# Splitting the second FFN product's left operands in place, inside the last pair of the first product, with the stores between them on ScalarE's queue

## The chip, the cores and the metric

The kernel runs on one core of a Trainium2 chip. The metric is the time of one execution in device microseconds (us); each number below is a median of single executions or comes from the profile of one of them. The engines are named as the profile names them: PE is TensorE (matmuls), PEld its weight loads, DVE is VectorE, ACT is ScalarE, POOL is GpSimd and SP is SyncE, which only issues DMA transfers. "SPq" and "ACTq" are DMA issues of SP and ACT.

## The reference

One layer of an encoder over 1024 tokens of width 1024, all in float32:

```
xn = rmsnorm(h); proj = xn @ w_in
h  = h + concat(windowed attention(proj), gated DeltaNet(proj)) @ w_out
hn = rmsnorm(h)
h  = h + square(relu(hn @ w_ffn_in)) @ w_ffn_out      # 1024 -> 4096 -> 1024
out = rmsnorm(h)
```

Only the FFN line, the second from last, is touched by the change: the first product `hn @ w_ffn_in`, its activation, and the second product with `w_ffn_out`.

## The kernel before

*Arithmetic.* TensorE multiplies float32 through operands that are split in two: a high part, which ACT makes by a cast (L119), and a low part, raw minus high, which POOL or DVE makes by a subtraction (L120). One product is then three matmuls (`mm3`, L124 to L126): high by high, high by low, low by high. A matmul here is a 128 by 128 weight against 512 columns.

*Seven products instead of eight.* Both FFN products are cut in 2 by 2 blocks and done by a Strassen-Winograd scheme: seven block products P1 to P7 of sums and differences of the blocks, whose results are added up afterwards. `SECOND` gives the order in which the second product does them: P1, P2, P6, P5, P7, P3, P4.

*First product.* It runs over 16 pairs g (a pair is 256 of the 4096 hidden features). `columns` loads a pair's weights, forms their combinations on DVE (L1020 to L1028) and splits them. `pair_products` does the seven products, 12 matmuls each, so 84 a pair, against the normed tokens X, whose 28 split tiles (`B11`, `B21` and so on, four each) hold all 28 buffers of the pool `pg` until the last pair has used them. Results go from PSUM through ACT (copy, L1049) and DVE (additions, L1044) to the activation: relu and square on ACT (L1054, L1055). DVE then forms the left operands that the second product will want (L1098 to L1106), and `keep` (L1060) stores the seven of a pair to a tensor `sd` in device memory: 112 stores of 256 KB, issued by SP.

*Second product.* It runs over 4 chunks n (a chunk is four pairs k) times 7 products: 28 steps of 48 matmuls. `second_operands` prepares a step. For each k it loads the left operand from `sd` into a `pt` buffer (L1132), has ACT cast it and DVE subtract it into a `pg` tile, and forms and splits the right operand from `w_ffn_out`: the combinations T1 (L1137), T2 (L1139), T3 (L1142) and N4 (L1143) on DVE, the cast on ACT, the low part on POOL. `second_products` does the matmuls, in groups of 12 for each of four PSUM banks, and adds each bank to a tile of h (L1170). The tag `psA` has four banks, which P1 and P6 use, then P7 and P4, then the next chunk's P1; `psB` has the other four, for P2, P5 and P3.

*Buffers.* `pg` 28, `pt` 12, `wr` 4, `wh` 3, `wl` 3, `sc` 4 per partition, and a new tile waits until the one that had the buffer before was last used.

*The order of the work.* The code is written in program order, product by product; a scheduler then reorders the instructions of each engine by a simulated time line, and each engine works through its own list in order. So the emission order in Python is an input of the order on the chip, not the order itself. In the code before, the last pair (g = 15) is written whole, then `prepare(0)` (the operands of step 0), then eight loads of h, 512 KB each (L1308). From there each step is written behind the preparation of the next.

Of the kernel before, what the change touches and what calls it, by code (L numbers as in the profile page):

```python
# [9 lines left out]
F32 = mybir.dt.float32  # L10
F32R = mybir.dt.float32r
# [66 lines left out]
class Block:  # L78
# [979 lines left out]
    def keep(self, g, p, t):  # L1058

        self.nc.sync.dma_start(out=self.sd[g, SECOND.index(p)], in_=t)  # L1060
# [11 lines left out]
    def pair_products(self, g, ops):  # L1072
# [7 lines left out]
        self.keep(g, "P1", a11)  # L1080
        self.product(a, ops, "P6", False)
        u2 = self.copied(a)
        c = self.ps(tag)
# [12 lines left out]
        self.keep(g, "P4", a22)  # L1096
        s1, s2, s4 = self.pt(), self.pt(), self.pt()
# [13 lines left out]
    def load_second(self, n):  # L1111

        out = []
        for k in range(4):
            g = 4 * n + k
            r = []
            for i in range(2):
                t = (self.wr, self.wh, self.wl, self.sc)[(2 * k + i) % 4]((P, 2, HALF), F32)
                f = (2 * g + i) * P
                self.nc.sync.dma_start(out=t, in_=self.io["w_ffn_out"][0, f:f + P, :].rearrange("p (h c) -> p h c", h=2))  # L1120
                r.append(t)
            out.append({"B11": r[0][:, 0], "B12": r[0][:, 1], "B21": r[1][:, 0], "B22": r[1][:, 1]})
        return out

    def second_operands(self, n, w2, p):

        nc, v = self.nc, self.nc.vector
        left, right = [], []
        for k in range(4):
            b = w2[k]  # L1130
            raw = self.pt()
            nc.sync.dma_start(out=raw, in_=self.sd[4 * n + k, SECOND.index(p)])  # L1132
            s, t = self.pg((P, 2, HALF), F32R), self.pg((P, 2, HALF), F32R)
            self.split(raw, s[:, 0], s[:, 1], v)
            if p == "P6":
                b["T1"] = b["B11"]
                v.tensor_tensor(out=b["T1"], in0=b["B12"], in1=b["B11"], op=ALU.subtract)  # L1137
                b["T2"] = self.pt()
                v.tensor_tensor(out=b["T2"], in0=b["B22"], in1=b["T1"], op=ALU.subtract)  # L1139
            if p == "P5":  # L1140
                b["T3"], b["N4"] = b["B12"], b["B21"]
                v.tensor_tensor(out=b["T3"], in0=b["B22"], in1=b["B12"], op=ALU.subtract)  # L1142
                v.tensor_tensor(out=b["N4"], in0=b["B21"], in1=b["T2"], op=ALU.subtract)  # L1143
            self.split(b[SECOND_RIGHT[p]], t[:, 0], t[:, 1])
            left.append(s)
            right.append(t)
        return left, right

# [76 lines left out]
    def phases(self):  # L1225
# [60 lines left out]
        rest[0]("P6", "P5", "P4")  # L1286
        for g in range(ng):
            if g == 0:
# [3 lines left out]
            else:  # L1292
                w2 = self.load_second(0)
            self.pair_products(g, cols.pop(g))
        steps = [(n, p) for n in range(ng // 4) for p in SECOND]
        ops, banks = {}, {}

        def prepare(i):
            nonlocal w2
            n, p = steps[i]  # L1300
            if p == "P1" and n:
                w2 = self.load_second(n)
            ops[i] = self.second_operands(n, w2, p)

        prepare(0)
        for t in range(NT):
            self.h[t] = self.pg((P, D))
            nc.sync.dma_start(out=self.h[t], in_=self.hd[t])  # L1308
        self.u2 = [self.pg((P, 2, HALF)) for _ in range(2)]
        for i, (n, p) in enumerate(steps):  # L1310
            if i + 1 < len(steps):
                prepare(i + 1)
            last = n == ng // 4 - 1
# [24 lines left out]
```

## Time and profile before

| | |
|---|---|
| median of 3 runs | 1277.7 us (1276.8 to 1280.23) |
| profiled execution | 1276.97 us, span 1275.3 us, mean granted clock of TensorE 0.981 |
| busy, share of the span | PE 1207.9 us (95%), DVE 860.6 (67%), ACT 613.6 (48%), POOL 580.9 (46%) |
| last matmul of the first product starts / second product starts | 940.07 / 949.83 us |
| last matmul starts | 1266.57 us |

How to read it: the span runs from the first to the last instruction of the profiled execution, and all times are counted from its start. An engine with a share of 95% can bound the kernel only as long as it is busy; so the stretches in which it is not are what a change can win, or lose. "PEclk" is the clock that was granted to TensorE, as a part of full speed (1.00 is 2.4 GHz, 0.5 would be 1.2 GHz). A wait is written as who waited, in which line, for whom.

### The profile page before, as it was taken

Reading aid. Unit: us, or ns where it says so; the run is one execution under the profiler, and the core shown is the slowest. Engines: PE = TensorE matmul, PEld = TensorE weight load, DVE = VectorE, ACT = ScalarE, POOL = GpSimd, SP = SyncE. Lnnn points to the kernel's source line nnn. Section 1 sums busy time; section 2 is a strip of 40 time slices with the busy share of each in tenths; the row PEclk is TensorE's granted clock in tenths of the full one; section 3 lists DMA queues with packets and bytes.
Section 4 is the critical chain, followed back from the end, with each engine's and each line's share of the span. In section 5 each row is a group of like instructions: output and inputs, shape, how many; then the busy total and the mean of one; then the engine's idle time right before and its main releaser. Section 6 shows DMA issues by size and latency. Waiting matters only on the chain. (4 is left out here: it accounts for less than half of the span.)

```text
span 1275.3 us, 18723 instructions
## 1 busy us (share of the span) xinstructions
PE 1207.9 (95%) x6482; PEld 972.6 (76%) x6482; DVE 860.6 (67%) x1534; ACT 613.6 (48%) x1347; POOL 580.9 (46%) x486
## 2 busy tenths in 40 slices
PE   6999999999899999999699999999957999999997
PEld 5778777778667778878488888888845888888886
DVE  5667676882488986675865455354459697887976
ACT  6455688244566662123655454454443443333343
POOL 5364221343432234233664453543526565565695
PEclk9999999899899999999899999999979999999999
DMA  6134444332946577123134444444685636444313
GB/s 234 51 119 134 116 151 174 116 106 70 237 127 173 166 233 266 64 93 131 35 126 154 141 157 149 141 149 163 212 304 198 226 110 198 124 133 132 104 38 132
DMA packets 120480, 187.64 MB, mean 147 GB/s; under 512 B 10915, under 2 KB 64288, under 8 KB 120385
## 3 DMA queue, kind: packets, MB, share of 16 engines
q1 hardware_dynamic: 111684, 181.95, 43.5%
q0 software_dynamic: 8448, 4.20, 1.8%
q8 instruction: 51, 0.84, 0.3%
q14 instruction: 44, 0.36, 0.1%
q10 hardware_dynamic: 253, 0.30, 0.1%
HBM read 122.39 MB, written 63.49 MB: 146 GB/s over the span
## 5 line engine op out<-in xcount | busy, mean ns | idle before, releaser
L124 PE MATMUL psA<-pg,wh 128*128 128x512 f32 x416 | 167.9, 404 | 2.7 <-ACT pt L458 2.2
L125 PE MATMUL psA<-pg,wh 128*128 128x512 f32 x416 | 166.7, 401 | 0.3 <-POOL pg L949 0.3
L126 PE MATMUL psA<-pg,wl 128*128 128x512 f32 x416 | 167.0, 401 | 0.0
L119 ACT CAST pg<-pt 128x512 fp32r<-128x512 f32 x128 | 76.4, 617 | 165.9 <-PE psA L126 63.5
L120 DVE TENSOR_TENSOR pg<-pt,pg 128x512 fp32r<-128x512 f32 x112 | 133.9, 1217 | 26.3 <-ACT pg L119 25.6
L120 POOL TENSOR_TENSOR wl<-wr,wh 128x512 fp32r<-128x512 f32 x44 | 70.5, 1625 | 153.6 <-ACT wh L119 153.6
L120 POOL TENSOR_TENSOR wh<-wr,wh 128x512 fp32r<-128x512 f32 x32 | 47.1, 1491 | 141.6 <-ACT wh L119 133.9
L1054 ACT ACTIVATE pt<-pt 128x512 f32<-128x512 f32 x64 | 40.4, 632 | 145.4 <-DVE pt L1044 145.4
L124 PE MATMUL psA<-pg,pg 128*128 128x512 f32 x256 | 100.4, 397 | 9.4 <-ACT pg L119 9.4
L126 PE MATMUL psA<-pg,pg 128*128 128x512 f32 x256 | 100.7, 394 | 4.0 <-DVE pg L120 4.0
L125 PE MATMUL psA<-pg,pg 128*128 128x512 f32 x256 | 100.5, 393 | 0.0
L124 PEld LDWEIGHTS psA<-pg,wh 128*128 128x128 f32 x416 | 79.2, 190 | 22.2 <-ACT pt L458 2.4
L125 PEld LDWEIGHTS psA<-pg,wh 128*128 128x128 f32 x416 | 79.3, 191 | 20.5 <-issue 0.9
L126 PEld LDWEIGHTS psA<-pg,wl 128*128 128x128 f32 x416 | 79.2, 190 | 18.6
L126 PE MATMUL psB<-pg,pg 128*128 128x512 f32 x192 | 74.9, 391 | 3.2 <-DVE pg L120 3.2
L125 PE MATMUL psB<-pg,pg 128*128 128x512 f32 x192 | 74.7, 389 | 0.0
L124 PE MATMUL psB<-pg,pg 128*128 128x512 f32 x192 | 74.7, 389 | 0.0
L1044 DVE TENSOR_TENSOR pt<-psB,pt 128x512 f32<-128x512 f32 x39 | 26.9, 690 | 63.8 <-PE psB L126 38.2
L1044 DVE TENSOR_TENSOR pt<-psA,pt 128x512 f32<-128x512 f32 x39 | 26.7, 689 | 59.2 <-PE psA L126 42.0
L119 ACT CAST wh<-wr 128x512 fp32r<-128x512 f32 x76 | 43.5, 623 | 45.1 <-PE psA L125 24.5
L124 PEld LDWEIGHTS psA<-pg,pg 128*128 128x128 f32 x256 | 49.0, 192 | 19.9 <-ACT pg L119 9.8
L126 PEld LDWEIGHTS psA<-pg,pg 128*128 128x128 f32 x256 | 48.7, 190 | 15.5 <-DVE pg L120 5.3
(376 smaller groups left out, 3344.3 us busy)
## 6 DMA issues: line engine op xcount, KB each, us to landing
sd<-pt SPq DMA_DIRECT2D x112, 256.0 KB, 2.2
pt<-sd SPq DMA_DIRECT2D x112, 256.0 KB, 3.0
wr<-in_w_ffn_in SPq DMA_DIRECT2D x32, 512.0 KB, 3.7
wr<-in_w_in SPq DMA_DIRECT2D x22, 512.0 KB, 5.0
pg<-in_x SPq DMA_DIRECT2D x16, 512.0 KB, 5.0
sc<-kvd SPq DMA_DIRECT2D x14, 512.0 KB, 4.2
kvd<-pt SPq DMA_DIRECT2D x16, 256.0 KB, 2.7
atd<-pt SPq DMA_DIRECT2D x16, 256.0 KB, 2.0
```

The costliest lines, as they stand in the source:

```text
L119: nc.scalar.copy(out=h, in_=raw)
L120: (eng or nc.gpsimd).tensor_tensor(out=l, in0=raw, in1=h.bitcast(F32), op=ALU.subtract)
L124: nc.tensor.matmul(ps, wh, xh, start=first, stop=False, skip_group_check=onto)
L125: nc.tensor.matmul(ps, wh, xl, start=False, stop=False, skip_group_check=onto)
L126: nc.tensor.matmul(ps, wl, xh, start=False, stop=last, skip_group_check=onto)
L1044: self.nc.vector.tensor_tensor(out=out, in0=in0, in1=in1, op=ALU.add)
L1054: self.nc.scalar.activation(out=c, in_=c, func=AF.Relu)
```

## The change

Four edits:

1. `keep` issues its stores from ACT's queue instead of SP's.
2. `second_operands` loads a left operand straight into the low half of its `pg` tile and splits it there, with no `pt` buffer: ACT casts the low half into the high half, DVE subtracts in place. The lefts of all four k are written ahead of the rights. The new lines are L1135 (load), L1136 (cast), L1137 (subtraction); T1, T2, T3 and N4 are L1144, L1146, L1149 and L1150 now.
3. `pair_products` takes hooks, called after its P2, P6 and P3. In the last pair `prepare(0)` is written behind P2, the other half of the weights and the first loads of h behind P6, and `prepare(1)` behind P3. The weights of a chunk are loaded in two parts: part 0 into the four `wr` buffers, part 1 into `wh`, `wl` and two `sc`.
4. h is loaded by 16 quarters of 256 KB (L1159): one group of four in the last pair, the others at steps 1, 2 and 3. Its additions are L1182 now.

```diff
     def keep(self, g, p, t):
-        self.nc.sync.dma_start(out=self.sd[g, SECOND.index(p)], in_=t)
+        self.nc.scalar.dma_start(out=self.sd[g, SECOND.index(p)], in_=t)
...
-    def pair_products(self, g, ops):
+    def pair_products(self, g, ops, then={}):
...
         self.keep(g, "P1", a11)
+        if "P2" in then:
+            then["P2"]()
         self.product(a, ops, "P6", False)
         u2 = self.copied(a)
+        if "P6" in then:
+            then["P6"]()
...
         self.keep(g, "P4", a22)
+        if "P3" in then:
+            then["P3"]()
...
-    def load_second(self, n):
+    def load_second(self, n, part):
         out = []
         for k in range(4):
...
+            t = (self.wr if part == 0 else (self.wh, self.wl, self.sc, self.sc)[k])((P, 2, HALF), F32)
+            f = (2 * (4 * n + k) + part) * P
...
     def second_operands(self, n, w2, p):
...
         for k in range(4):
+            s = self.pg((P, 2, HALF), F32R)
+            raw = s[:, 1].bitcast(F32)
+            nc.sync.dma_start(out=raw, in_=self.sd[4 * n + k, SECOND.index(p)])
+            nc.scalar.copy(out=s[:, 0], in_=raw)
+            v.tensor_tensor(out=s[:, 1], in0=raw, in1=s[:, 0].bitcast(F32), op=ALU.subtract)
+            left.append(s)
+        for k in range(4):
             b = w2[k]
-            raw = self.pt()
-            nc.sync.dma_start(out=raw, in_=self.sd[4 * n + k, SECOND.index(p)])
-            s, t = self.pg((P, 2, HALF), F32R), self.pg((P, 2, HALF), F32R)
-            self.split(raw, s[:, 0], s[:, 1], v)
+            t = self.pg((P, 2, HALF), F32R)
...
+    def load_h(self, half, side):
+        sl = slice(side * HALF, (side + 1) * HALF)
+        for t in range(4 * half, 4 * half + 4):
+            self.nc.sync.dma_start(out=self.h[t][:, sl], in_=self.hd[t][:, sl])
...
+        def after_p6():
+            self.h[0:4] = [self.pg((P, D)) for _ in range(4)]
+            self.load_h(0, 0)
+            for a, b in zip(w2[0], self.load_second(0, 1)):
+                a.update(b)
+        def after_p3():
+            self.h[4:8] = [self.pg((P, D)) for _ in range(4)]
+            self.u2 = [self.pg((P, 2, HALF)) for _ in range(2)]
+            prepare(1)
...
-                w2 = self.load_second(0)
-            self.pair_products(g, cols.pop(g))
...
-        prepare(0)
-        for t in range(NT):
-            self.h[t] = self.pg((P, D))
-            nc.sync.dma_start(out=self.h[t], in_=self.hd[t])
-        self.u2 = [self.pg((P, 2, HALF)) for _ in range(2)]
+                w2[0] = self.load_second(0, 0)
+                then = {"P2": lambda: prepare(0), "P6": after_p6, "P3": after_p3}
+            self.pair_products(g, cols.pop(g), then)
         for i, (n, p) in enumerate(steps):
-            if i + 1 < len(steps):
+            if 0 < i and i + 1 < len(steps):
                 prepare(i + 1)
+            if 0 < i < 4:
+                self.load_h(*((1, 1), (0, 1), (1, 0))[i - 1])
```

The order on TensorE at the point where the two kernels part, before: behind pair 14's P6 (the bank `psA_1499`) come pair 15's P5 (`psB_1522`) and P7 (`psB_1524`).

```order
L126 MATMUL psA_1499_8500<-pg_1197_6383,sc_1473_8334 128x512
L124 MATMUL psB_1522_8683<-pg_1167_6276,sc_1495_8488 128x512
L125 MATMUL psB_1522_8683<-pg_1167_6276,sc_1495_8488 128x512
L124 MATMUL psB_1524_8698<-pg_1113_6090,wh_1496_8491 128x512
L125 MATMUL psB_1524_8698<-pg_1113_6090,wh_1496_8491 128x512
L126 MATMUL psB_1524_8698<-pg_1113_6090,wh_1496_8491 128x512
```

And now; `psB_1534` and `psB_1536` are pair 15's P5 and P7 here, and `psA_1555` is the first bank of the second product's P1, with left operands and right operands both in `pg` tiles.

```order
L126 MATMUL psA_1499_8500<-pg_1197_6383,sc_1473_8334 128x512
L124 MATMUL psA_1555_8828<-pg_1521_8677,pg_1517_8661 128x512
L125 MATMUL psA_1555_8828<-pg_1521_8677,pg_1517_8661 128x512
L126 MATMUL psA_1555_8828<-pg_1521_8677,pg_1517_8661 128x512
L124 MATMUL psA_1555_8828<-pg_1522_8680,pg_1518_8665 128x512
L125 MATMUL psA_1555_8828<-pg_1522_8680,pg_1518_8665 128x512
L126 MATMUL psA_1555_8828<-pg_1522_8680,pg_1518_8665 128x512
L124 MATMUL psB_1534_8719<-pg_1167_6276,sc_1495_8488 128x512
L125 MATMUL psB_1534_8719<-pg_1167_6276,sc_1495_8488 128x512
L124 MATMUL psB_1536_8734<-pg_1113_6090,wh_1496_8491 128x512
```

The second product's first matmuls have moved ahead of pair 15's P5 and P7; between its later products stand the rest of P1 and, from 108 rows further down, P2.

The order on ACT between pair 14 (tiles `pt_8242` to `pt_8287`) and pair 15 (`pt_8363`, `psB_8349` is a PSUM bank of the pair; the `CAST` rows split weights), before:

```order
L1054 ACTIVATE pt_8287<-pt_8287 128x512
L1055 ACTIVATE pt_8287<-pt_8287 128x512
L1054 ACTIVATE pt_8242<-pt_8242 128x512
L1055 ACTIVATE pt_8242<-pt_8242 128x512
L1049 COPY pt_8363<-psB_8349 128x512
L1054 ACTIVATE pt_8363<-pt_8363 128x512
L119 CAST wh_8340<-wr_8319 128x512
L119 CAST wh_8477<-wr_8470 128x512
L1055 ACTIVATE pt_8363<-pt_8363 128x512
L119 CAST sc_8334<-wr_8319 128x512
L119 CAST sc_8337<-pt_8323 128x512
```

And now; `sd` is the tensor in device memory, so the L1060 rows are the stores.

```order
L1060 DMA sd<-pt_8292 128x512
L1054 ACTIVATE pt_8242<-pt_8242 128x512
L1060 DMA sd<-pt_8287 128x512
L1055 ACTIVATE pt_8242<-pt_8242 128x512
L1060 DMA sd<-pt_8293 128x512
L1060 DMA sd<-pt_8242 128x512
L1049 COPY pt_8363<-psB_8349 128x512
L1060 DMA sd<-pt_8294 128x512
L1054 ACTIVATE pt_8363<-pt_8363 128x512
L119 CAST wh_8340<-wr_8319 128x512
L119 CAST wh_8477<-wr_8470 128x512
L1055 ACTIVATE pt_8363<-pt_8363 128x512
```

Between the pair's last relu (`pt_8242`) and the next pair's copy there stand three stores and the square now, where the square stood alone; a fourth store stands between the copy and the next relu.

The order on DVE at the boundary from chunk 0 to chunk 1, before: L1170 adds a PSUM bank to h, L120 is a left operand's low part, L1137, L1139 and L1142 are T1, T2 and T3 of chunk 1.

```order
L1170 TENSOR_TENSOR pg_8790<-pg_8790,psB_9120 128x512
L1137 TENSOR_TENSOR wr_9348<-wr_9348 128x512
L1139 TENSOR_TENSOR pt_9543<-wh_9350,wr_9348 128x512
L1142 TENSOR_TENSOR wr_9348<-wh_9350,wr_9348 128x512
L1170 TENSOR_TENSOR pg_8792<-pg_8792,psB_9134 128x512
L1170 TENSOR_TENSOR pg_8794<-pg_8794,psB_9148 128x512
L120 TENSOR_TENSOR pg_9374<-pt_9372,pg_9374 128x512
L120 TENSOR_TENSOR pg_9382<-pt_9380,pg_9382 128x512
L1170 TENSOR_TENSOR pg_8796<-pg_8796,psB_9162 128x512
L1137 TENSOR_TENSOR wl_9352<-wl_9352 128x512
```

And now (L1182 adds a bank to h, L1137 is a left operand's low part, L1144, L1146 and L1149 are T1, T2 and T3):

```order
L1182 TENSOR_TENSOR pg_8703<-pg_8703,psB_9108 128x512
L1137 TENSOR_TENSOR pg_9348<-pg_9348 128x512
L1182 TENSOR_TENSOR pg_8704<-pg_8704,psB_9122 128x512
L1182 TENSOR_TENSOR pg_8705<-pg_8705,psB_9136 128x512
L1182 TENSOR_TENSOR pg_8706<-pg_8706,psB_9150 128x512
L1144 TENSOR_TENSOR wr_9328<-wr_9328 128x512
L1137 TENSOR_TENSOR pg_9352<-pg_9352 128x512
L1146 TENSOR_TENSOR pt_9526<-wh_9336,wr_9328 128x512
L1149 TENSOR_TENSOR wr_9328<-wh_9336,wr_9328 128x512
L1144 TENSOR_TENSOR wr_9330<-wr_9330 128x512
L1137 TENSOR_TENSOR pg_9356<-pg_9356 128x512
```

The first T1, with T2 and T3 behind it, has moved behind all four additions from `psB`, and the low part of the third left operand (`pg_9382` before, `pg_9352` now) has moved with them. On the same engine, in the last pair, the first two T1 of chunk 0 now stand among L1020 to L1028 of pair 15, one ahead of L1027 and one ahead of L1028.

## Rows read from the trace of the kernel before

**Rows 1.** Busy time by stretch: stretch, each engine's busy time (instructions), PEclk, DMA share, GB/s

```profile
core 0: us, PE busy (x) PEld busy (x) DVE busy (x) ACT busy (x) POOL busy (x), PEclk, DMA share, GB/s
864.00:896.00 32.00, 32.00 (x139) 25.87 (x138) 17.65 (x24) 16.70 (x30) 12.05 (x9) 1.00 0.44 156
925.60:949.83 24.23, 10.88 (x39) 7.74 (x37) 9.47 (x15) 8.56 (x15) 0.00 (x0) 0.79 0.82 273
949.83:986.00 36.17, 28.91 (x106) 21.70 (x107) 35.82 (x34) 15.90 (x30) 26.28 (x16) 0.91 0.64 233
1216.00:1248.00 32.00, 32.00 (x143) 26.47 (x142) 24.58 (x25) 11.96 (x22) 32.00 (x22) 1.00 0.03 9
```

**Rows 2.** TensorE's waits, 910 to 1010: for whom; total us, times, longest

```profile
PE psA L124 <- ACT pg L119: 9.4, 1, 9.4
PE psA L126 <- DVE pg L120: 4.0, 2, 3.2
PE psB L126 <- DVE pg L120: 3.2, 3, 1.3
PE psB L124 <- ACT pt L1049: 2.6, 1, 2.6
PE psB L124 <- DVE pt L1044: 1.4, 1, 1.4
```

**Rows 3.** TensorE in order of time: start, duration, line, what, [idle before, releaser]

```profile
920.27 0.39 PE L124 MATMUL psA<-pg,wl 128*128 128x512 f32 x1
...
925.63 0.39 PE L126 MATMUL psA<-pg,sc 128*128 128x512 f32 x1
...
949.83 2.07 PE L124 MATMUL psA<-pg,pg 128*128 128x512 f32 x4 [9.36 <-ACT pg L119]
...
1264.76 0.39 PE L124 MATMUL psA<-pg,pg 128*128 128x512 f32 x1
...
1266.57 0.39 PE L126 MATMUL psA<-pg,pg 128*128 128x512 f32 x1
```

**Rows 4.** SP's DMA issues in order of time, at the seam

```profile
940.92 3.40 SPq L1060 DMA_DIRECT2D sd<-pt  x5
```

**Rows 5.** The chain of waits in order of time: start, duration, what

```profile
944.41 4.21 DMA pt<-sd
```

**Rows 6.** All engines in order of time, around 890, one pair's chain

```profile
889.86 0.57 ACT L1049 COPY pt<-psB 128x512 f32<-128x512 f32 x1
...
891.20 0.68 DVE L1044 TENSOR_TENSOR pt<-psB,pt 128x512 f32<-128x512 f32 x1
...
894.60 0.62 ACT L119 CAST sc<-pt 128x512 fp32r<-128x512 f32 x1
...
895.64 0.40 PE L124 MATMUL psA<-pg,sc 128*128 128x512 f32 x1
```

**Rows 7.** DMA issues by source line: duration in ns min/median/max, first and last start

```profile
L1060 SPq DMA_DIRECT2D sd<-pt x112: 319/320/1165, 647.0 to 943.3; - x112
...
L144 ACTq DMA_DIRECT2D sc<-in_conv_w x1: 662/662/662, 0.8 to 0.8; - x1
```

**Rows 8.** DVE and POOL in order of time, 949 to 966

```profile
949.85 1.28 POOL L120 TENSOR_TENSOR pg<-wr,pg 128x512 fp32r<-128x512 f32 x1 [30.31 <-ACT pg L119]
951.09 1.74 POOL L120 TENSOR_TENSOR pg<-wl,pg 128x512 fp32r<-128x512 f32 x1
...
951.61 1.77 DVE L1137 TENSOR_TENSOR wr<-wr 128x512 f32<-128x512 f32 x1
...
965.74 0.68 DVE L1137 TENSOR_TENSOR wl<-wl 128x512 f32<-128x512 f32 x1
```

**Rows 9.** DVE in order of time, boundary of chunks 0 and 1

```profile
1022.37 0.69 DVE L1137 TENSOR_TENSOR wr<-wr 128x512 f32<-128x512 f32 x1 [0.59 <-POOL pg L120]
...
1028.59 0.67 DVE L1170 TENSOR_TENSOR pg<-pg,psB 128x512 f32<-128x512 f32 x1
...
1038.52 0.68 DVE L1170 TENSOR_TENSOR pg<-pg,psA 128x512 f32<-128x512 f32 x1
```

**Rows 10.** DMA issues by kind: queue, count, KB each, median us to landing

```profile
pg<-hd SPq DMA_DIRECT2D x8, 512.0 KB, 9.3
```

More of the change, by code (lines that the diff above doesn't have):

```diff
@@ L1108, in pair_products @@
         self.keep(g, "P3", s4)
-    def load_second(self, n):
+    def load_second(self, n, part):
         out = []
         for k in range(4):
[L1115 to L1122, printed above, removed]
+            t = (self.wr if part == 0 else (self.wh, self.wl, self.sc, self.sc)[k])((P, 2, HALF), F32)
+            f = (2 * (4 * n + k) + part) * P
+            self.nc.sync.dma_start(out=t, in_=self.io["w_ffn_out"][0, f:f + P, :].rearrange("p (h c) -> p h c", h=2))
+            out.append({f"B{part + 1}{h + 1}": t[:, h] for h in range(2)})
         return out
@@ L1144, in second_operands @@
             self.split(b[SECOND_RIGHT[p]], t[:, 0], t[:, 1])
-            left.append(s)
             right.append(t)
         return left, right
+    def load_h(self, half, side):
+        sl = slice(side * HALF, (side + 1) * HALF)
+        for t in range(4 * half, 4 * half + 4):
+            self.nc.sync.dma_start(out=self.h[t][:, sl], in_=self.hd[t][:, sl])
     def second_products(self, n, p, left, right, banks, last):
@@ L1286, in phases, with prepare @@
         rest[0]("P6", "P5", "P4")
+        steps = [(n, p) for n in range(ng // 4) for p in SECOND]
+        ops, banks, w2 = {}, {}, {}
+        def prepare(i):
+            n, p = steps[i]
+            if p == "P1" and n:
+                w2[n] = self.load_second(n, 0)
+                for a, b in zip(w2[n], self.load_second(n, 1)):
+                    a.update(b)
+            ops[i] = self.second_operands(n, w2[n], p)
+        def after_p6():
+            self.h[0:4] = [self.pg((P, D)) for _ in range(4)]
+            self.load_h(0, 0)
+            for a, b in zip(w2[0], self.load_second(0, 1)):
+                a.update(b)
+        def after_p3():
+            self.h[4:8] = [self.pg((P, D)) for _ in range(4)]
+            self.u2 = [self.pg((P, 2, HALF)) for _ in range(2)]
+            prepare(1)
         for g in range(ng):
+            then = {}
             if g == 0:
@@ L1292, in phases @@
             else:
-                w2 = self.load_second(0)
-            self.pair_products(g, cols.pop(g))
[L1295 to L1303, printed above, removed]
-        prepare(0)
-        for t in range(NT):
-            self.h[t] = self.pg((P, D))
-            nc.sync.dma_start(out=self.h[t], in_=self.hd[t])
-        self.u2 = [self.pg((P, 2, HALF)) for _ in range(2)]
+                w2[0] = self.load_second(0, 0)
+                then = {"P2": lambda: prepare(0), "P6": after_p6, "P3": after_p3}
+            self.pair_products(g, cols.pop(g), then)
         for i, (n, p) in enumerate(steps):
-            if i + 1 < len(steps):
+            if 0 < i and i + 1 < len(steps):
                 prepare(i + 1)
+            if 0 < i < 4:
+                self.load_h(*((1, 1), (0, 1), (1, 0))[i - 1])
             last = n == ng // 4 - 1
```

## The prediction

> **What bounds the kernel now.** I read the page first: TensorE is busy for 95% of the span, so the kernel can only gain where TensorE stands still or runs slowly. I then looked for the places by the busy time in stretches [rows 1]. From 864 to 896, in the first FFN product, and from 1216 to 1248, in the second, TensorE is busy for all 32.00 us at a granted clock of 1.00. Only between 925.6 and 986 is it not: 24.23 − 10.88 and 36.17 − 28.91 make 20.6 us of idle time, and the clock reads 0.79 and 0.91, a mix of its two levels (1.2 and 2.4 GHz). This is the seam between the two products. TensorE's waits around it give the causes [rows 2]: 9.4 us for the ACT cast of the second product's first left operand, 4.0 and 3.2 for low parts from DVE, 2.6 and 1.4 inside pair 15 for its own results.
>
> What the seam costs in all follows from the matmuls in order of time [rows 3]. In the first product 23 steps from 920.27 to 925.63 are 0.233 us each. Behind 925.63 there are 36 matmuls of it left; at that pace they would end at 934.25, and the second product would start there. It starts at 949.83: 15.6 us lost. Its 28 × 48 = 1344 matmuls at 0.226 us (8 steps from 1264.76 to 1266.57) need 304.2 us, and it takes 1266.80 − 949.83 = 317.0: 12.8 us lost. Together 28.4 us, of which 20.6 is idle time and the rest falls to matmuls at the lower clock level after the gaps.
>
> Why the second product starts so late is in SP's order and in the chain of waits [rows 4, 5]: SP issues five stores of pair 15 from 940.92 for 3.40 us, and only behind them the first load of `sd`, at 944.41; it takes 4.21, and the cast and TensorE follow.
>
> **The change part by part.** I take the profiled execution, 1276.97 us with a span of 1275.3; the median of the runs shown, 1277.7, is 0.7 higher.
>
> *Emission inside the last pair.* In the order of the changed kernel six matmuls of the second product's P1 stand ahead of the first ones of pair 15's P5 and P7, and the rest of P1 and P2 between pair 15's remaining products: 96 matmuls × 0.226 = 21.7 us of work that depends on nothing pair 15 makes late. It lies in the place of the 2.6, the 1.4 and the 9.4 us waits, and while TensorE stays busy I expect the clock to stay at 1.00, as in the full rows of [rows 1]. The left operands of chunk 0 come from pairs 0 to 3, stored long ago, and their buffers are those of X's `B11` and `B21`, free once pair 15's P1 and P2 are done. All of it covered: −28.4.
>
> What is given back, in four places:
>
> (a) *112 stores leave SP for ACT.* SP's issues do not gate the pairs, since TensorE is busy throughout 864 to 896. ACT gets seven issues a pair in the middle of a chain. In the pair around 890 [rows 6] the copy ends at 889.86 + 0.57 = 890.43, and the addition that takes it starts on DVE at 891.20, 0.77 later; the cast at 894.60 ends at 895.22, and TensorE uses such an operand at 895.64, 0.42 later. In the new order three stores stand ahead of the copy and a fourth behind it. An issue takes SP 0.32 us (median of 112); ACT's first DMA of the kernel took 0.66 [rows 7]. At 0.32, 3 × 0.32 − 0.77 = 0.19 us late, inside the 0.42; at 0.66, 1.98 − 0.77 − 0.42 = 0.8 a pair. I go by the 112, with 0.15 a pair for the copies in pairs with less room: × 14 = 2 us (0 to 11).
>
> (b) *The DVE work of the seam.* With the sixteen subtractions T1 to N4 and the left low parts, DVE is busy for 35.82 of 36.17 us up to 986 [rows 1]. One takes 0.68 us alone and 1.77 beside POOL, whose own go from 1.28 to 1.74 [rows 8]. The change removes none of it; it starts sooner, but TensorE needs it sooner too, and two T1 now stand between the subtractions of pair 15's own columns. Two at 1.77, less six matmuls × 0.226, are up to 2.2 us for pair 15's operands. For the products behind P2 the nearest rows are the waits of before, 4.0 + 3.2. With T1 starting up to 20 us sooner I take half of these 7.2 and all of the 2.2, 6 us (0 if all is ready ahead, 10 if both come whole).
>
> (c) *Three chunk boundaries.* Before, the first T1 of chunk 1 stands on DVE behind one addition to h from psB and starts at 1022.37; now it stands behind all four, the last of which starts at 1028.59 and ends at 1029.26 [rows 9]. By then DVE had done three T operations and one left low part that are now still to come: four of 0.68 to 1.77 each [rows 8], 2.7 to 7.1 us, of which I take the middle, 4.5, since POOL works part of the time. Behind the T operations wait P4's additions to h. The one at 1038.52 ends at 1039.20 [rows 9], and the next chunk's P1 wants that bank at 1266.80 − 1008 × 0.226 + 12 × 0.226 = 1041.7, so 2.5 us of it is slack. 2.0 a boundary, × 3 = 6 us (0 to 14, the latter with all four at 1.77 beside POOL).
>
> (d) *The last chunk.* POOL is busy for all 32.00 us from 1216 to 1248 [rows 1]. Right low parts that come one bank later there, 12 × 0.226 = 2.7 us, have nowhere to catch up: 2 us (0 to 3).
>
> *h in quarters*: the seam's loads of 512 KB take 9.3 us to land (median of 8) [rows 10], and a quarter is first used a whole step, 48 × 0.226 = 10.9 us, behind its issue or later. The loads of left operands now wait for their pg buffer, two steps ahead, 22 us against the 4.21 of [rows 5]. Both at 0, covered by TensorE's own steps; a left that did come late would cost its load, 4 to 5 us, once. The tail behind the last matmul, 1275.3 − 1266.8 = 8.5, stays.
>
> Sum: −28.4 + 2 + 6 + 6 + 2 = −12.4, so 1264.6, and on the median's scale 1265.
>
> In (b) the trace shows both sides lengthened, 0.68 to 1.77 and 1.28 to 1.74 [rows 8]. Here the Trainium skill speaks against the change ("SBUF — State Buffer", "Who interferes with whom"): a DVE instruction with two SBUF inputs and a GpSimd instruction that reads SBUF share a port pair as an exclusive lock, and the loser blocks for the whole instruction. By that, one of each in turn would take 0.68 + 1.28 = 1.96 us; the rows have 1.77, a little less than the full lock. With 1.96 the sixteen operations would add 16 × 0.19 = 3 us to (b), and the sum would be 1268.
>
> **The rivals.**
> A. The forecast: the gaps go, some 16 us come back. About 1265 (1258 to 1272).
> B. All is covered. For it: DVE is busy for only 17.65 of 32 us in the pairs [rows 1], so that the last pair has room for the T operations. Against it: DVE is full for the 36 us behind. With (a) to (d) at 0 to 4 in all, 1249 to 1254.
> C. DVE is the bound of the seam: the 12.8 us of the second product stay and only 15.6 is gained. With (a), (c) and (d) at 2 + 6 + 2 the time is 1272; with (c) at 12, near its end, it is 1278, no change. For it: the 35.82 us of DVE work [rows 1], which the change leaves whole. Here too belongs that the change does not do what it says: TensorE gets to P1 and P2 early and finds no operands.
> D. The stores on ACT stretch each of 14 pairs. At 0.66 us an issue, the fourth store counted too, 4 × 0.66 − 0.77 − 0.42 = 1.45 us × 14 = 20; with (b) to (d) at 14 that is 34 against 28.4, so 1283, slower. It decides from about 1.3 us a pair. For it: ACT's first issue, and that ACT must wait in order for every tile it stores. Against it: SP's median of 0.32, and ACT busy for only 16.70 of 32 us [rows 1].
>
> **How the numbers follow.** A 0.60, B 0.15, C 0.18, D 0.07. The likeliest is 1265. For 8 in 10, A whole, half of B and most of C: 1252 to 1277. About 0.3% (3.8 us) is what a measurement of this kernel can tell from no change: faster is below 1273.9, all of A and B and a third of C, 0.81; the same goes up to 1281.5, two thirds of C and a little of D, 0.13; slower 0.06.
>
> **What would show it.** Right: TensorE busy without a hole where the seam's first gap was, the clock at 1.00 and the 9.4 us wait gone; some 6 us of waits on DVE low parts left; new waits of TensorE behind additions to h at three boundaries, about 2 us each; the pairs up to 925 at 84 × 0.233 = 19.6 us. Wrong: waits of TensorE in every pair on ACT's casts or copies (D), over 8 us of waits on DVE at the second product's P6 and P5 (C), none at the boundaries (B).

## The result, and the profile after

The changed kernel takes 1264.76 us (median of 4, 1262.38 to 1267.07) against 1278.97 us beside it; the ratio is 0.990 with a 95% interval of 0.988 to 0.992 (the two medians alone give 0.989). Run again later on the same chip as the last experiment, it stands at 0.991 (0.989 to 0.992). 1265 was forecast, inside 1252 to 1277, and "faster" had 0.81.

Each time below is of one profiled execution, and in these the way up to the FFN, which no edit here touches, varies by more than most effects: the first product's first copy by ACT (L1049) starts between 635.84 and 643.21 us in the twelve of them. So I cut every execution at two marks, the first and the 30th of the 34 copies, and at the last matmul: "pairs" is from mark to mark, "rest" from the 30th copy to the start of the last matmul. The 30th copy is pair 13's second (two from `psA`, pair 14's, and two from `psB`, pair 15's, follow it); the expectations below call it the copy of pair 14. The marks, of the kernel before and of the changed one (start, duration, line):

```profile
636.48 0.59 ACT L1049 COPY pt<-psA 128x512 f32<-128x512 f32 x1
...
896.69 0.58 ACT L1049 COPY pt<-psB 128x512 f32<-128x512 f32 x1
```

```profile
639.33 0.60 ACT L1049 COPY pt<-psA 128x512 f32<-128x512 f32 x1
...
900.59 0.58 ACT L1049 COPY pt<-psB 128x512 f32<-128x512 f32 x1
```

So the pairs took 260.2 us of before and 261.3 now; the rest took 1266.57 − 896.69 = 369.9 [rows 3] and takes 1256.70 − 900.59 = 356.1. The profiled 1267.07 us is 9.9 less than the profiled 1276.97, and the FFN in it is 12.7 us shorter; the other 2.9 were lost ahead of it.

Busy time by stretch now (columns as in [rows 1]); what was the seam lies between 905 and 990:

```profile
core 0: us, PE busy (x) PEld busy (x) DVE busy (x) ACT busy (x) POOL busy (x), PEclk, DMA share, GB/s
...
896.00:928.00 32.00, 28.82 (x123) 22.66 (x122) 22.01 (x26) 18.80 (x33) 19.66 (x14) 1.00 0.65 204
928.00:960.00 32.00, 29.71 (x118) 22.81 (x117) 18.23 (x26) 13.38 (x24) 9.27 (x7) 0.95 0.85 294
960.00:992.00 32.00, 31.31 (x135) 24.79 (x134) 30.06 (x31) 18.06 (x33) 20.84 (x13) 1.00 0.83 281
1024.00:1056.00 32.00, 31.74 (x140) 25.91 (x140) 30.76 (x37) 12.96 (x23) 20.64 (x12) 1.00 0.28 97
1216.00:1248.00 32.00, 31.17 (x134) 24.38 (x133) 23.32 (x24) 12.46 (x21) 29.55 (x24) 1.00 0.23 76
```

TensorE is idle for 3.2, 2.3 and 0.7 us where it was for 20.6 [rows 1], and the clock reads 1.00, 0.95 and 1.00 instead of 0.79 and 0.91. New are small losses further on: 0.3 us around a chunk boundary (1024 to 1056) and 0.8 in the last chunk (1216 to 1248), where before it was busy for all 32.00 in both stretches. The waits of TensorE from 850 on, which answer to [rows 2]:

```profile
PE psB L124 <- ACT sc L119: 2.0, 1, 2.0
PE psB L125 <- POOL pg L120: 1.4, 2, 0.7
PE psA L124 <- ACT pt L1049: 1.2, 1, 1.2
PE psB L126 <- DVE pg L1137: 1.2, 2, 0.9
PE psA L124 <- DVE pg L1182: 0.9, 3, 0.3
PE psB L124 <- ACT pg L1136: 0.7, 1, 0.7
PE psA L125 <- POOL pg L120: 0.4, 1, 0.4
```

The 9.4 and the 2.6 us waits are gone; eleven of 0.3 to 2.0 us have come. The matmuls behind which they stand, in order of time, answer to [rows 3]:

```profile
916.90 0.50 PE L124 MATMUL psA<-pg,sc 128*128 128x512 f32 x1 [1.22 <-ACT pt L1049]
...
923.32 0.50 PE L124 MATMUL psB<-pg,sc 128*128 128x512 f32 x1 [1.96 <-ACT sc L119]
...
946.95 0.40 PE L124 MATMUL psB<-pg,pg 128*128 128x512 f32 x1
...
949.03 0.51 PE L125 MATMUL psB<-pg,pg 128*128 128x512 f32 x1 [0.72 <-POOL pg L120]
...
950.45 0.50 PE L124 MATMUL psB<-pg,pg 128*128 128x512 f32 x1 [0.68 <-ACT pg L1136]
...
952.06 0.50 PE L126 MATMUL psB<-pg,pg 128*128 128x512 f32 x1 [0.88 <-DVE pg L1137]
...
1256.70 0.39 PE L126 MATMUL psA<-pg,pg 128*128 128x512 f32 x1
```

With what each gap costs behind it (a first matmul of 0.34 instead of 0.23, and 0.43 at the lower clock, behind 952.40) this is the account of the loss that is left: 1.5 us at 916.90, 2.2 at 923.32, 5.0 in the 24 matmuls of the second product's P2 from 946.95 to 957.43, 1.5 at its P6 and P5, 3 × 0.55 = 1.7 at the chunk boundaries, 2.4 in the last chunk. That is 14.3, and by the forecast's bound, 369.9 − 28.4 = 341.5, the rest should lose 356.1 − 341.5 = 14.6.

### The profile page after: what moved, and what is told of

It reads as the page before. It is cut to its first block, busy times and chain, and to the rows that moved or that the text cites. A ratio compares the mean times of both kernels' runs of the same rounds, so it can differ in the third digit from the quotient of the medians.

```text
span 1265.4 us, 18552 instructions
## 1 busy us (share of the span) xinstructions
PE 1210.0 (96%) x6482; PEld 970.6 (77%) x6482; DVE 859.0 (68%) x1534; ACT 621.4 (49%) x1347; POOL 577.7 (46%) x486
## 4 chain that ended last, share of the span: by engine, by line
PE 58%; DVE 7%; DMA 3%; issue 2%; POOL 1%; ACT 1%; ACTq 0%; POOLq 0%; DVEq 0%
PE psA L124 8%; PE psA L125 8%; PE psA L126 8%; PE psB L126 7%; PE psB L124 7%; PE psB L125 7%; PE psB L796 5%; DMA pg<-sd 2%; PE psA L584 2%; PE psA L573 2%; DVE pg L1137 1%; PE psA L544 1%; DVE pt L1146 1%; POOL pg L120 1%; PE psA L545 1%
## 5 line engine op out<-in xcount | busy, mean ns | idle before, releaser
L120 POOL TENSOR_TENSOR wl<-wr,wh 128x512 fp32r<-128x512 f32 x44 | 70.7, 1629 | 153.3 <-ACT wh L119 153.2
L1137 DVE TENSOR_TENSOR pg<-pg 128x512 fp32r<-128x512 f32 x112 | 123.2, 1135 | 18.1 <-ACT pg L1136 18.1
L120 POOL TENSOR_TENSOR wh<-wr,wh 128x512 fp32r<-128x512 f32 x32 | 47.6, 1508 | 132.1 <-ACT wh L119 124.4
L125 PE MATMUL psA<-pg,pg 128*128 128x512 f32 x256 | 99.8, 391 | 0.4 <-POOL pg L120 0.4
L124 PE MATMUL psA<-pg,pg 128*128 128x512 f32 x256 | 99.0, 391 | 0.9 <-DVE pg L1182 0.9
L126 PE MATMUL psA<-pg,pg 128*128 128x512 f32 x256 | 99.7, 389 | 0.0
L120 POOL TENSOR_TENSOR pg<-wr,pg 128x512 fp32r<-128x512 f32 x48 | 73.4, 1559 | 50.8 <-ACT pg L119 50.8
L1136 ACT CAST pg<-pg 128x512 fp32r<-128x512 f32 x112 | 66.8, 620 | 38.4 <-DMA pg<-sd 32.0
L124 PEld LDWEIGHTS psA<-pg,pg 128*128 128x128 f32 x256 | 48.0, 188 | 12.6 <-DVE pg L1182 2.2
```

The lines of the kernel that those rows point to most:

```text
L120: (eng or nc.gpsimd).tensor_tensor(out=l, in0=raw, in1=h.bitcast(F32), op=ALU.subtract)
L124: nc.tensor.matmul(ps, wh, xh, start=first, stop=False, skip_group_check=onto)
L125: nc.tensor.matmul(ps, wh, xl, start=False, stop=False, skip_group_check=onto)
L126: nc.tensor.matmul(ps, wl, xh, start=False, stop=last, skip_group_check=onto)
L1136: nc.scalar.copy(out=s[:, 0], in_=raw)
L1137: v.tensor_tensor(out=s[:, 1], in0=raw, in1=s[:, 0].bitcast(F32), op=ALU.subtract)
```

## The experiments

All twelve executions in one table; the ratio is to the kernel before, with its 95% interval.

| kernel | pairs, us | rest, us | ratio |
|---|---|---|---|
| before | 260.2 | 369.9 | 1 |
| changed | 261.3 | 356.1 | 0.990 (0.988 to 0.992) |
| changed, once more | 260.9 | 354.3 | 0.991 (0.989 to 0.992) |
| 1: changed, all stores on SP | 259.9 | 351.3 | 0.987 (0.985 to 0.990) |
| 2: before, only the stores on ACT | 260.8 | 364.4 | 0.999 (0.997 to 1.000) |
| 3: changed, first loads of h later | 261.0 | 351.3 | 0.988 (0.986 to 0.990) |
| 4: changed, pair 15's stores on SP | 260.9 | 353.1 | 0.991 (0.988 to 0.993) |
| 5: changed, no T1 to N4 in chunk 0 | 260.9 | 351.7 | 0.987 (0.984 to 0.989) |
| 6: 1 and 3 together | 259.9 | 352.3 | 0.985 (0.983 to 0.988) |
| 7: 1, left and right in turn | 260.2 | 348.7 | 0.984 (0.982 to 0.985) |
| 8: 1, h's first four tiles whole and early | 259.9 | 349.1 | 0.985 (0.983 to 0.986) |
| 9: combined | 259.9 | 345.1 | 0.982 (0.980 to 0.983) |

The intervals of the ratios overlap for many of these; where two lie close, I go by "pairs" and "rest", which take out what varies ahead of the FFN, and by the waits. Two executions of the changed kernel differ by 1.8 us in the rest; less than that between two kernels is not told apart here unless a wait shows it. "Pairs" and "rest" are of one execution of each kernel, the ratio is of all its runs; where they disagree in size, the text says so.

**1. All stores back on SP.**

```diff
-        self.nc.scalar.dma_start(out=self.sd[g, SECOND.index(p)], in_=t)
+        self.nc.sync.dma_start(out=self.sd[g, SECOND.index(p)], in_=t)
```

> The changed kernel with its 112 stores back on SP; everything else of the change stays. Theory (transfers): the move of the stores is worth little by itself. The pairs get back the 0.74 us by which they drifted in the changed kernel (copies 2.85 us behind those of before at the first pair, 3.59 at the last), ACT is no longer held in the last pair (its copy waited 5.7 us behind stores), but SP has five stores ahead of the left loads again, 3.4 us as before. Net -2 to +3 us against the changed kernel, ratio to before 0.988 to 0.992. Rival (the move of the queue is what makes the gain): the 3.4 us and the 9.4 us wait behind them come back, +6 us or more, ratio 0.995 or more.

The theory's size was wrong: the rest is 4.8 us shorter than in the changed kernel and the pairs 1.4 shorter (3.0 and 1.0 against its second execution). The rival, that the gain comes by the queue, is refuted: without it the gain is larger. What ACT does in the changed kernel from 936 to 946 (ACTq is a DMA issue by ACT; a merged row runs from the first of its issues to the end of the last):

```profile
936.70 0.63 ACT L1055 ACTIVATE pt<-pt 128x512 f32<-128x512 f32 x1 [1.27 <-DVE pt L1105]
937.53 5.44 ACTq L1060 DMA_DIRECT2D sd<-pt  x4
943.02 0.59 ACT L1049 COPY pt<-psB 128x512 f32<-128x512 f32 x1 [5.69 <-DMA sd<-pt]
...
945.08 0.61 ACT L119 CAST pg<-wh 128x512 fp32r<-128x512 f32 x1
```

Four stores take 5.44 us from the first to the last, where an issue by itself is 0.33, and the copy behind them waits 5.7. One by one, the second, third and fourth:

```profile
938.78 0.33 ACTq L1060 DMA_DIRECT2D sd<-pt  x1
...
941.21 0.33 ACTq L1060 DMA_DIRECT2D sd<-pt  x1
...
942.65 0.33 ACTq L1060 DMA_DIRECT2D sd<-pt  x1
```

Their tiles were ready by 938.90, when DVE's L1113 ends. What holds them is in the trace's semaphore events: the DMA issues of SP and ACT in this program share eight completion semaphores, and an issue stands behind the landing of the transfer that had its semaphore before (of 284 such pairs in the changed kernel whose landing can be told, no issue starts ahead of it). The three wait for two of SP's loads, issued at 932.35 (h) and 933.83 (`w_ffn_out`), which took 6.4 and 7.3 us to land, and for ACT's own store of 936.33; each starts 0.08 us behind that landing. The cast at 945.08 is what POOL waits for, idle for ten microseconds, before it makes the right low parts of P2:

```profile
945.77 1.53 POOL L120 TENSOR_TENSOR pg<-wh,pg 128x512 fp32r<-128x512 f32 x1 [10.02 <-DMA sd<-pt]
```

TensorE's wait on POOL at 949.03 is for these. With the stores on SP it is busy for all 25 us of the same stretch, with as much to transfer (changed kernel first, then this one; columns as in [rows 1]):

```profile
930.00:955.00 25.00, 22.71 (x92) 17.22 (x91) 15.41 (x21) 10.31 (x19) 7.27 (x6) 0.96 0.98 343
```

```profile
930.00:955.00 25.00, 25.00 (x110) 20.38 (x109) 16.41 (x23) 14.07 (x24) 6.84 (x5) 1.00 1.01 375
```

The DMA engines are full in both, 0.98 and 1.01, and the loads of left operands take 6.0 us to land here (one of eight, the only one whose landing the profile tells) and 4.6 to 8.2 there (three of eight). So full transfers alone do not cost the 5.0 us of P2. Here the waits for landings fall on SP: of pair 14's last five stores one, at 939.03, starts right behind a landing, at 938.97, and ACT's copy, at 936.97, waits for none. Not all of it is ACT's hold either: in experiments 4 and 5, which have the same hold and hardly a wait on left operands, P2 loses 2.2 and 3.2 us, with waits on POOL alone. The rest of the 5.0 are the lefts, waited for at 950.45 and 952.06, and the lower clock behind them.

**2. Only the stores moved, in the kernel before.**

```diff
-        self.nc.sync.dma_start(out=self.sd[g, SECOND.index(p)], in_=t)
+        self.nc.scalar.dma_start(out=self.sd[g, SECOND.index(p)], in_=t)
```

> The kernel before with one line changed: the stores go out by ACT's queue. Theory: -3 us at the seam (the first left load no longer stands behind five stores that take SP 3.4 us), +0.7 us in the pairs: ratio 0.998. Rival (the queue makes the gain): ratio 0.993 or less. Rival (stores stretch ACT's chain, as D in the prediction): ratio above 1.003 and waits of TensorE on ACT in the pairs.

As the theory had it, in the main: 0.9987, with no change just inside the interval (0.9972 to 1.0002) and the bounds of both rivals outside, and the pairs 0.55 us longer. At the old seam the stores stood ahead of the loads on SP [rows 4], and there the move shortens the first wait from 9.4 to 6.8 us, but the copy of pair 15 now waits longer (3.5 instead of 2.6 [rows 2]):

```profile
PE psA L124 <- ACT pg L119: 6.8, 1, 6.8
PE psB L126 <- DVE pg L120: 4.0, 1, 4.0
PE psB L124 <- ACT pt L1049: 3.5, 1, 3.5
```

So the same edit is worth −4.9 us by itself in the profiled executions (rest and pairs together), 2.2 us between the medians of all runs, and +4 to +6 beside the other three: the emission inside the last pair takes the loads out from behind the stores anyway, and puts loads that are long to land ahead of ACT's stores. In experiment 2 the transfers that had the semaphores of pair 14's last stores and of pair 15's before had landed when these came up, and the stores waited for their tiles alone.

**3. The first loads of h later.**

```diff
-            self.load_h(0, 0)
...
-            if 0 < i < 4:
-                self.load_h(*((1, 1), (0, 1), (1, 0))[i - 1])
+            if i < 4:
+                self.load_h(*((0, 0), (1, 1), (0, 1), (1, 0))[i])
```

> The changed kernel with the first four loads of h (1 MB in all) written at the second product's first step, behind the last pair, instead of inside it. Theory (transfers): in the changed kernel the 16 DMA engines are busy for 0.94 to 1.04 of the time from 930 to 955, and P2's left operands take 7 to 8 us to land instead of 2.8; 1 MB at the 400 GB/s of that stretch is 2.6 us, so these land some 2.5 us sooner and of the 5.0 us that TensorE loses in P2 about half goes: -2 to -3 us against the changed kernel, ratio 0.988. Rival (DVE's subtractions T1 to N4 are what TensorE waits for): no change, ratio 0.990. Either way additions to h may come late once, 0 to 2 us.

The rest is 351.3, 3.0 to 4.8 us less, so more than expected and not nothing, as the rival would have it. But it is not that left operands land sooner and nothing else: ACT's order is drawn up anew with it, and its copy, at 942.05, no longer stands behind a row of held stores:

```profile
940.50 0.93 ACTq L1060 DMA_DIRECT2D sd<-pt  x2
...
942.05 0.58 ACT L1049 COPY pt<-psB 128x512 f32<-128x512 f32 x1
```

TensorE loses nothing in P2 here. What lets the stores through is in the trace: for those of 937.77 and 940.50 the transfers that had their semaphores before had landed by 932.68 and 937.00, and the second starts when its tile is done, by DVE's L1106 at 940.46. Whether 1 MB less to transfer would have done it in the old order, this run does not tell; the DMA share from 930 to 955 is still 0.93.

**4. Pair 15's stores on SP.**

```diff
-        self.nc.scalar.dma_start(out=self.sd[g, SECOND.index(p)], in_=t)
+        (self.nc.sync if g == 15 else self.nc.scalar).dma_start(out=self.sd[g, SECOND.index(p)], in_=t)
```

> The changed kernel with the seven stores of the last pair alone on SP; TensorE's order is the same as in the changed kernel. Theory: ACT's copy of pair 15 no longer waits 5.7 us behind its stores, so the POOL low parts of P2 (which waited 10.0) come 5 us sooner and TensorE's waits on POOL and ACT at 949 to 951 go; the waits on left operands that are still in flight stay or grow, since SP now has the stores ahead of these loads. -1 to +3 us against the changed kernel. Rival (ACT held by its stores is the cause of the 5.0 us lost in P2): -4 to -5 us, ratio 0.986.

A miss in its design, and telling for it. The copy waits as before, for 5.3 us, behind four stores that take 5.11:

```profile
935.03 5.11 ACTq L1060 DMA_DIRECT2D sd<-pt  x4
940.18 0.58 ACT L1049 COPY pt<-psB 128x512 f32<-128x512 f32 x1 [5.34 <-DVE pg L1182]
```

The profile names an addition to h as what ended the wait; by time it is the fourth store, which ends at 940.14. The run was meant to take this wait away. Since pair 15's stores are gone from ACT here, the stores that hold it are pair 14's, which this edit leaves on ACT. The rest, 353.1, is between the changed kernel's and that of experiment 1, and the ratio is that of the changed kernel.

**5. No T1 to N4 in chunk 0.**

```diff
-            if p == "P6":
+            if p == "P6" and n == 0:
+                b["T1"], b["T2"], b["T3"], b["N4"] = b["B11"], b["B22"], b["B12"], b["B21"]
+            elif p == "P6":
...
-            if p == "P5":
+            if p == "P5" and n > 0:
```

> The changed kernel without the sixteen subtractions T1 to N4 of chunk 0: its products take the raw blocks of w_ffn_out instead, so that part of the computation is left out. Everything else stays, the other three chunks too. Theory (term (b) of the prediction, DVE's subtractions hold up the seam): TensorE's wait on the ACT cast at 923 (2.0 us, behind DVE's L1027, which stood behind a T1 of 1.77) goes, and so do the waits at the second product's P6 and P5 (some 1.5 us with the restarts): from the copy of pair 14 to the last matmul 352 to 353 us, against 356.1 in the changed kernel. The 5.0 us lost in P2 stay. Rival (the casts of pair 15 are late for another reason, ACT's stores among them): the wait at 923 stays at 2.0 and the stretch at 355 to 356.

The theory holds for the waits that it names. In the changed kernel DVE runs a T1 (L1144, 1.78 us) ahead of L1027 (1.77), and the cast at 922.13 and the matmul at 923.32 follow:

```profile
918.57 1.78 DVE L1144 TENSOR_TENSOR wr<-wr 128x512 f32<-128x512 f32 x1
920.27 1.77 DVE L1027 SCALAR_TENSOR_TENSOR wr<-pt,wr 128x512 f32<-128x512 f32 x1
```

Without T1 the wait on that cast is 0.2 us instead of 2.0, and those at P6 and P5 are gone; the ones in P2 and at the boundaries stay:

```profile
PE psB L125 <- POOL pg L120: 2.8, 5, 0.7
...
PE psA L124 <- DVE pg L1184: 0.9, 3, 0.3
...
PE psB L124 <- ACT sc L119: 0.2, 1, 0.2
```

The rest is 351.7, 2.7 to 4.4 us less and just under the 352 to 353 expected: DVE's share of the seam, and in it some of the loss in P2, which is 3.2 us here and did not stay at 5.0.

**6. Experiments 1 and 3 together.**

> The changed kernel with both of the edits that shortened it in the profile: stores back on SP, and the first four loads of h behind the last pair. From the copy of pair 14 to the last matmul each alone went from 356.1 to 351.3 us. Theory (both take away the same thing, ACT held by its own stores while the transfers are crowded, which cost 5.0 us in P2): together no more than either, 350 to 352, and the pairs at 259.9 as with SP. Rival (two separate gains): 346 to 348.

352.3, no more than either alone, and TensorE loses nothing in P2 in any of the three: they take away the same thing, and the rival of two separate gains falls. With the stores on SP the later loads bring only new waits, of 1.0 us each on a cast and on POOL at P6.

**7. Left and right in turn, as before, on top of 1.**

```diff
             left.append(s)
-        for k in range(4):
             b = w2[k]
```

> Stores on SP, and left and right operands written in turn for each k as in the kernel before, instead of all four lefts ahead of the rights. On DVE the first T1 of the next chunk then stands behind one addition from psB again, and no T1 of chunk 0 stands between L1022 and L1028 of pair 15. Theory (term (c): lefts first push the T operations back and with them P4's additions): TensorE's three waits on additions to h at the boundaries (0.26 to 0.3 each, some 0.55 with the restart) go, -1.7 us; the wait on the cast in pair 15 (2.7 in the kernel with the stores on SP, 3.0 and 1.6 of lower clock behind it) goes or falls under 1: from the copy of pair 14 to the last matmul 346 to 348 us instead of 351.3. Rival (the order of the operands does not matter, or the lefts come late instead): 351 or more, with waits on DVE's left low parts.

```profile
PE psA L126 <- DVE pg L1137: 2.2, 1, 2.2
PE psB L124 <- ACT sc L119: 1.3, 1, 1.3
PE psB L126 <- DVE pg L1137: 0.5, 1, 0.5
```

The waits on additions to h (0.9 in all in the changed kernel) are gone, as term (c) wanted; so is the loss of the last chunk. So both come from writing the four lefts ahead of the rights. But chunk 0 now pays at its P6, 2.2 us and a stretch at the lower clock, the cast in pair 15 still costs 1.3 us, which I had expected gone or under 1, and the rest is 348.7, a little above what I expected.

**8. h's first four tiles whole and early, on top of 1.**

```diff
             self.load_h(0, 0)
+            self.load_h(0, 1)
...
-            if 0 < i < 4:
-                self.load_h(*((1, 1), (0, 1), (1, 0))[i - 1])
+            if i == 1:
+                self.load_h(1, 1)
+                self.load_h(1, 0)
```

> Stores on SP, and all of h's first four tiles loaded inside the last pair (2 MB instead of 1 MB), the other four whole at the second step. Theory (crowded transfers cost only by way of ACT's queue): with the stores on SP there is room, 351 to 353 us from the copy of pair 14 to the last matmul. Rival (transfers by themselves set P2's start): 1 MB more at 400 GB/s is 2.6 us more, 353.5 to 355, with TensorE waiting on left operands (ACT cast or DVE low part behind a load of sd).

349.1: 1 MB more in the fullest stretch costs nothing. The 2.2 us less than in experiment 1 lie in pair 15, not where h is used: the wait on the cast in pair 15 is 2.2 us instead of 2.7, and the eight matmuls at the lower clock behind it (0.43 instead of 0.23 each, 1.5 us) did not come this time. The transfers by themselves do not set P2's start, and to hold half of h's first four tiles back brings nothing when SP issues the stores. The loads are of 256 KB here too; their size was not tested.

**9. What the runs point to, in one kernel**: stores on SP, h as in 8, lefts first in chunk 0 and in turn in chunks 1 to 3.

```diff
-        self.nc.scalar.dma_start(out=self.sd[g, SECOND.index(p)], in_=t)
+        self.nc.sync.dma_start(out=self.sd[g, SECOND.index(p)], in_=t)
...
-        for k in range(4):
+        def load_left(k):
...
+        for k in range(4 if n == 0 else 0):
+            load_left(k)
         for k in range(4):
+            if n:
+                load_left(k)
...
```

> What the runs point to, in one kernel: stores on SP, h's first four tiles whole inside the last pair, left operands of chunk 0 ahead of the rights, and left and right in turn for chunks 1 to 3. Theory: from the kernel with halves of h early (349.1 us from the copy of pair 14 to the last matmul) go the three waits at the chunk boundaries (1.7 us with restarts) and the loss of the last chunk (2.4), which were both gone with operands in turn: 345 us, ratio to before 0.981. The wait on the cast in pair 15 (2.2) stays. Rival (the gains do not add, since the order is drawn up anew): 348 to 350, ratio 0.984.

1253.45 us (1252.05 to 1257.48), ratio 0.982: faster than both. The rest is 345.1, as worked out, one wait is left of the eleven, and the clock reads 1.00 through what was the seam:

```profile
PE psB L124 <- ACT sc L119: 2.6, 1, 2.6
```

```profile
928.00:960.00 32.00, 32.00 (x141) 26.19 (x140) 24.69 (x37) 19.37 (x34) 11.14 (x8) 1.00 1.01 363
960.00:992.00 32.00, 32.00 (x143) 26.48 (x142) 26.46 (x27) 15.86 (x30) 22.43 (x15) 1.00 0.65 222
```

It is the cast of pair 15 behind a T1 of chunk 0 on DVE. **The changed kernel once more**, beside it:

> The changed kernel once more, unaltered, on the same chip as the combined one. Theory: 355 to 357 us from the copy of pair 14 to the last matmul, the pairs at 261, with ACT's copy behind its stores again waiting over 4 us in the last pair; ratio 0.990. Rival (the held stores were an accident of one execution): 351 to 352 us and no such wait.

354.3 is just under the 355 that I had set; the held stores are there again, in the same place and of the same length:

```profile
935.68 5.67 ACTq L1060 DMA_DIRECT2D sd<-pt  x4
941.39 0.59 ACT L1049 COPY pt<-psB 128x512 f32<-128x512 f32 x1 [5.91 <-DMA sd<-pt]
```

## Why the prediction was right, and where it was not

*The term of −28.4.* Right. Experiment 9 comes to 345.1, within 3.6 us of the 341.5 at which all of it would be covered, and the clock reads 1.00 from 928 to 992 there. That the hooks bring it is read from TensorE's order and from the 9.4 us wait that is gone; no run takes the hooks out, or undoes the split in place, by itself.

*(a) The stores on ACT, 2 us.* Mis-sized: it costs 4.1 to 6.2 us (experiment 1, rest and pairs together; by the ratios 3.6 to 4.5). In the pairs I was near enough: 0.5 to 1.0 us from the first copy to the 30th, with no wait of TensorE up to 905, so rival D is refuted where it was put. What I missed is the place, and the kind. I priced a store by the time of its issue, 0.32 us, with 0.66 as the upper bound [rows 7], and had no term for what an issue waits for. In the changed kernel four issues of 0.33 took 5.44 us, because three of them waited for an earlier transfer to land; and 1.1 of the 1.5 us lost at 916.90 (0.4 in experiment 1) come with ACT's new order, in which stores that wait for their tiles, and a cast, stand ahead of pair 14's copy. Rival D had ACT held by its stores, but by long issues and in every pair. The issue times of before do not show this, and SP's five stores at the seam are no hint of it: of their 3.40 us [rows 4] none is a wait for an earlier transfer; two of the five waited for a result of DVE (L1099, L1100), and the last issue took 0.97. The order too was another at that place. The rows on ACT that are given ahead of the prediction as pair 14 to pair 15 are pair 12 to pair 13 (`sc_8334`, cast behind the copy, is an operand of pair 14's P6); at pair 15's copy five stores stand behind the last relu and ahead of the copy, not three.

*(b) The DVE work of the seam, 6 us.* Right in kind, too large: of the account above 2.2 us at 923.32 and 1.5 at P6 and P5 are DVE's, 3.7, and experiment 5 takes away 2.7 to 4.4. The 2.2 us for pair 15's operands behind two T1 is what I had; of the 7.2 us of waits on left low parts the half that I took was too much. Of the 6 us of waits on DVE low parts that I wanted to see, 1.2 are there (L1137).

*(c) The chunk boundaries, 6 us.* Right in kind (the waits on additions to h are there, and experiment 7 removes them), but 1.7 in size. The first T1 does stand behind the fourth addition from `psB`:

```profile
1013.83 0.69 DVE L1182 TENSOR_TENSOR pg<-pg,psB 128x512 f32<-128x512 f32 x1 [2.03 <-PE psB L126]
1014.50 1.76 DVE L1144 TENSOR_TENSOR wr<-wr 128x512 f32<-128x512 f32 x1
...
1020.19 0.68 DVE L1144 TENSOR_TENSOR wr<-wr 128x512 f32<-128x512 f32 x1
...
1032.41 0.67 DVE L1182 TENSOR_TENSOR pg<-pg,psA 128x512 f32<-128x512 f32 x1
```

It starts 0.67 us behind it, as the order said. I let four operations of up to 1.77 us push all that came after. Only the first three ran at 1.76 to 1.78. POOL had ended its run at 1019.12 and stood still until 1024.05, and from 1019.59 until 1026.2 DVE's operations took 0.68, so that all but 0.3 us was made up at the addition of 1032.41. DVE was not idle in between; POOL's pause, and the pace that it gives DVE, was missing in my sum.

*(d) The last chunk, 2 us.* 2.4, and by experiment 7 for the reason given.

*h in quarters and left loads, 0.* To spread h's loads is worth nothing (experiment 8). The left loads did come late. The chain of waits has 8.02 us for one of P2's, where I had 4.21 [rows 5], and 7.04 for another, which has the same semaphore and was issued when the first had landed:

```profile
934.26 8.02 DMA pg<-sd
942.30 7.04 DMA pg<-sd
```

I had priced that at 4 to 5 us once; in experiments 1 and 8, with the stores on SP, it is covered.

So the sum, 16 us given back, was right (14.6 in the rest and 1.0 in the pairs) by errors that cancel: (a) 2 to 4 too small, (b) 2 and (c) 4 too large. The mechanism of the gain and the time were right; that the four terms summed to the right size is luck, and the costliest edit was one that I had put among the cheapest.

*The lock of DVE and POOL.* The Trainium skill's rule ("SBUF — State Buffer", "Who interferes with whom") has the two engines exclude each other for a whole instruction; by it I estimated 1.96 us for one DVE and one POOL subtraction in turn. Beside the other either takes 1.7 to 1.8 us here, as before [rows 8]. My 1.96 added durations, and successive instructions overlap a little: from start to start it is 0.60 us for DVE and 1.25 for POOL alone, 1.85 in all, and 1.70 together. So the trace is near the rule, somewhat under it, and the rule's extra 3 us is not in the account above.

*The queue of the stores.* On the move itself the Trainium skill says ("DMA: Bandwidth & Descriptors", "Issuing engines are not separate DMA queues") that transfers started by different engines end up on the same 16 DMA engines, and that spreading the issues saves only the sequencer's time. Experiment 2 agrees: what the move gives there is SP's time, the first wait falling from 9.4 to 6.8 us. Beside the other edits it gives nothing, since with the stores on SP TensorE is busy through the seam's fullest 25 us (experiment 1), and the engine that takes the issues over pays with its waits.

## What to carry to other kernels

Before moving DMA issues to an engine that also computes, ask what each issue will wait for, and not only how long an issue takes: in this program an issue waits for its tile and for the earlier transfer that had its semaphore, and on a computing engine everything behind it waits too. When two edits attack the same wait, time each alone and both together; here one that gains 2 to 5 us alone, if anything, costs 4 to 6 beside the others. And when work is pushed back on an engine, look at the pace at which it will run there: three operations of 1.77 us were followed by a stretch at 0.68, and the backlog was made up.

## What was not expected of the hardware

A row of issues can be long with each issue short: ACT's four stores start at 937.53, 938.78, 941.21 and 942.65, up to 2.4 us apart, and take 0.33 us each; the longest single issue that the trace records for ACT is 0.67 us in this execution and 1.19 in the second one. The time lies between the issues, in the waits for landings that experiment 1 shows. The four executions with the hold (the changed kernel twice, experiments 4 and 5) have ten such stores, and each starts 0.08 us behind the landing that it waits for. Full DMA engines alone do not make the hold: with a share of 0.93 in experiment 3 ACT's stores are not held. They come in by making landings late, 6 to 7 us for the transfers that the stores waited for.

The way up to the FFN varies by 7.4 us (635.84 to 643.21) between executions of kernels that are the same up to there. Without a mark at its end, half of the effects above could not have been told from it.
